# Regrouping a head's preparation: queries beside the gate tiles, keys and values beside an output projection

## The chip, the cores and the metric

The kernel runs on one core of one Trainium2 chip. The time is the device time of the program in microseconds (us), median of the runs taken. TensorE (PE) multiplies, ScalarE (ACT) and VectorE (DVE) copy, scale and reduce, GpSimd (POOL) does some elementwise work from SBUF, SyncE (SP) issues most transfers. Each engine takes its instructions in one fixed order.

## The reference

One decoder layer on 1024 tokens of width 1024, in float32, batch 1. Two branches read the same normalised input, and their outputs are projected by one matrix:

```python
h = rms_norm(x, norm1_g) * (1.0 + scale1) + shift1
q_lat, kv_lat, k_rope, x_lru, g_lru = jnp.split(h @ w_in, IN_SPLITS, axis=-1)
attn = mla_attention(q_lat, kv_lat, k_rope, ...)   # 4 heads, q and k normalised and rotated
lru = rg_lru_branch(x_lru, g_lru, ...)             # convolution, gates, scan, times gelu(g_lru)
mixed = jnp.concatenate([rms_norm(attn, ...), rms_norm(lru, ...)], axis=-1)
x = x + gate1 * (mixed @ w_out)
h2 = rms_norm(x, norm2_g) * (1.0 + scale2) + shift2
x = x + gate2 * hierarchical_moe(h2, ...)          # 32 experts, 2 per token
```

A head's query comes from `q_lat` through `w_q_b`, its key and value from `kv_lat` through `w_kv_b`; `k_rope` is shared by the heads.

## The kernel before

Tokens are handled as 8 tiles of 128 rows. `w_in` is multiplied in twelve column tiles (`FT`), each in two halves of 512 tokens; a float32 product is made of three faster ones (`mm3`: high by high, high by low, low by high), so one half of a tile is 24 PE instructions of 512 columns named `pp`. The last four tiles (i = 8 to 11) are the gate tiles `gl`: `gl_steps` multiplies them, and `gelu` (L654) makes the gate, multiplies it into the recurrent output `lru[j]` on DVE (L655), squares it on ACT (L659), and adds the square into `sqL` on POOL (L660).

Then `l_pass` projects the recurrent half of the mixed rows with rows 512 to 1023 of `w_out`. `out_w` loads four blocks `wo` of `w_out`, multiplies each by the gate row `m_g1` on POOL (L1046, four instructions a block), and splits it into `woh` (ACT) and `wol` (DVE, L222). `norms` sums `sqL` on PE (`pc2`, L1059) and takes a reciprocal root in twelve tiny DVE instructions (`rsq`, L199 to L213), which end in `ivL`. Sixteen output tiles `pL` of 12 PE instructions follow; each is scaled by `ivL` and added to the input rows `xr` by one DVE instruction (L1082) that also frees the PSUM bank. `pL` has three banks. A second `out_w` prepares the other half of `w_out` beside it, for the attention's projection much later.

`prep(h, P)` prepares a head. Its key part multiplies the latent by `w_kv_b` (24 PE instructions `pkv`, L225 to L227), copies keys (`kraw`, ACT) and values (`v`, DVE), squares, sums and takes a reciprocal root (`ssk`, `ik`), scales the keys on POOL (L807, L810) and transposes them twice (`k_t`, PE `ptk` and `ptk2`) into `kTh`, `kTl` and `ks`. Its query part multiplies by `w_q_b` (`pq`, L820), squares and rotates, and transposes (`ptq`) into `qTh`, `qTl`, `qs`, `ql`; a third `rsq` gives the scale `scq`.

For head 0 the whole of `prep` is written beside the end of `gl_steps` and `l_pass`, in turns that `merge` sets by two step counts; heads 1 to 3 are prepared beside the attention of the head before:

```python
gl = chain(gl_steps(), l_pass())
for _ in range(OPT["gl0"]):
    next(gl)
merge((gl, OPT["glw"] - OPT["gl0"]), (prep(0, P), NPREP))
drain(gl)
```

The written order is only a wish: a scheduler of the framework, which also gives out the buffers, fixes each engine's order when the program is built. With `phase(1)` the PSUM banks are given out anew; the first scores `pS` (L932) of head 0's attention follow.

Of the kernel before, what the change touches and what calls it, by code (L numbers as in the profile page):

```python
# [9 lines left out]
F32 = mybir.dt.float32  # L10
F32R = mybir.dt.float32r
# [3 lines left out]
AF = mybir.ActivationFunctionType  # L15
OP = mybir.AluOpType
# [122 lines left out]
def layer(ctx, tc, A, out, dbg=None, stop=None):  # L139
# [10 lines left out]
    def blk(name, dt=F32):  # L150
        return big.tile([128, 1024], dt, name=name, tag="b", bufs=NBLK)
# [77 lines left out]
    def t3(ap, t):  # L229
        return ap.rearrange("p (t f) -> p t f", t=t)  # L230
# [542 lines left out]
    attn = [None] * 4  # L773
    sqA = None

    def prep(h, P):
        kTh, kTl, ks = blk("kTh", F32R), blk("kTl", F32R), blk("ks", F32R)
        vh = blk("v")
        kraw = blk("kraw")
        P.update(kTh=kTh, kTl=kTl, ks=ks, v=vh)  # L780
        lkh, lkl = latk
        ssk = sm.tile([128, NT], F32, name="ssk")
        sq = blk("sqh")
        for t0 in range(0, NT, 2):
            pkk = t3(bank("pkv"), 2)
            for a in range(2):
                ts_ = slice((t0 + a) * 128, (t0 + a) * 128 + 128)
                hs = slice(h * 256, h * 256 + 256)
                mm3(pkk[:, a], lkh[:, ts_], lkl[:, ts_], wkh[:, hs], wkl[:, hs], True, True)
            for a in range(2):  # L790
                rk = r_k[:, t0 + a:t0 + a + 1]
                tk = slice((t0 + a) * 128, (t0 + a) * 128 + 128)
                SC.activation(kraw[:, tk], pkk[:, a, :128], AF.Copy, scale=rk)
                if OPT["ssk"]:
                    SC.activation(sq[:, tk], pkk[:, a, :128], AF.Square, scale=rk, accum_out=ssk[:, t0 + a:t0 + a + 1])
                V.tensor_scalar(vh[:, tk], pkk[:, a, 128:], rk, None, op0=OP.mult)
            yield
        if not OPT["ssk"]:
            SC.activation(sq, kraw, AF.Square)
            V.tensor_reduce(ssk, t3(sq, NT), op=OP.add, axis=AX.X)  # L800
            yield
        V.tensor_add(ssk, ssk, ssr)
        yield
        ik = sm.tile([128, NT], F32, name="ik")
        yield from rsq(ik, ssk, 1.0 / 192, EPS, [128, NT])
        k3 = t3(kraw, NT)
        G.tensor_mul(k3, k3, ik[:, :, None].to_broadcast([128, NT, 128]))  # L807
        kp3 = t3(sq, NT)
        for r in range(2):
            G.tensor_mul(kp3[:, :, r * 64:r * 64 + 64], krr, ik[:, :, None].to_broadcast([128, NT, 64]))  # L810
        yield
        ssh = sm.tile([128, NT], F32, name="ssh")
        Q = {}
        qst = {}

        def q_mm(t0):
            pq = t3(bank("pq"), 2)[:, :, :192]
            for a in range(2):
                for k in range(2):
                    T.matmul(pq[:, a], latq[k][:, (t0 + a) * 128:(t0 + a) * 128 + 128], wq[k][:, h * 192:(h + 1) * 192],  # L820
                             start=(k == 0), stop=(k == 1))
            qnp = half("qnp").rearrange("p (c a d) -> p c a d", c=2, a=2)
            qn, qp = qnp[:, 0], qnp[:, 1]
# [12 lines left out]
            two_ = lambda v: v[:, :, None, :].to_broadcast([128, 2, 2, 64])
            V.tensor_add(qp.rearrange("p a (r d) -> p a r d", r=2), two_(qp[:, :, 64:]), two_(tm))
            if not OPT["ssh"]:
                V.tensor_reduce(ssh[:, t0:t0 + 2], sqh, op=OP.add, axis=AX.X)
            qst[t0] = qn, qp  # L840

        def q_t(t0):
            qn, qp = qst.pop(t0)
            if t0 % 4 == 0:
                Q.update({n: half(n, F32R) for n in ("qTh", "qTl", "qs", "ql")})
                for n in Q:
                    P[n, t0 // 4] = Q[n]
                G.memset(Q["ql"][64:].bitcast(F32), 0.0)
            pt = bank("ptq")
            for a in range(2):  # L850
                T.transpose(pt[:, a * 128:(a + 1) * 128], qn[:, a], ident)
            for a in range(2):
                T.transpose(pt[:, 256 + a * 128:256 + (a + 1) * 128], qp[:, a], ident)
            tv = slice((t0 % 4) * 128, (t0 % 4) * 128 + 256)
            split(pt[:, :256], Q["qTh"][:, tv], Q["qTl"][:, tv])
            SC.activation(Q["qs"][:, tv], pt[:, 256:], AF.Copy)
            V.tensor_sub(Q["ql"][:64, tv], pt[:64, 256:], Q["qs"][:64, tv])

        def k_t(c0):
            tv = slice(c0 * 128, c0 * 128 + 512)  # L860
            pt = bank("ptk")
            for a in range(4):
                T.transpose(pt[:, a * 128:(a + 1) * 128], k3[:, c0 + a], ident)
            split(pt, kTh[:, tv], kTl[:, tv], scale=gg)
            yield
            pt = bank("ptk2")
            for a in range(4):
                T.transpose(pt[:, a * 128:(a + 1) * 128], kp3[:, c0 + a], ident)
            SC.activation(ks[:, tv], pt, AF.Copy)
            V.tensor_sub(ks[64:, tv], pt[64:], ks[64:, tv])  # L870
            yield

        def scale():
            sq_ = smc.tile([128, NT], F32, name="scq", bufs=2)
            r2 = sm.tile([128, NT], F32, name="r2")
            V.tensor_mul(r2, r_q, r_q)
            yield
            V.tensor_mul(r2, r2, ssh)
            yield
            yield from rsq(sq_, r2, 1.0 / 192, EPS, [128, NT])  # L880
            V.scalar_tensor_tensor(sq_, sq_, SCALE, r_q, op0=OP.mult, op1=OP.mult)
            yield
            nsq = smc.tile([128, NT], F32, name="nscq", bufs=2)
            V.tensor_scalar(nsq, sq_, -1.0, None, op0=OP.mult)
            P.update(scq=sq_, nscq=nsq)

        def turns():
            q_mm(0)
            yield
            for t0 in range(2, NT, 2):  # L890
                q_mm(t0)
                yield
                if t0 < NT - 2:
                    q_t(t0 - 2)
                    yield
                if t0 == 4:
                    yield from k_t(0)

        yield from turns()
        sc_ = scale()  # L900
        for f in (lambda: q_t(NT - 4), lambda: q_t(NT - 2)):
            f()
            yield
            for _ in range(4):
                next(sc_)
                yield
        for _ in k_t(4):
            yield
            for _ in range(3):
                next(sc_, None)  # L910
                yield
        yield from sc_
# [101 lines left out]

    def gl_steps():
        for i in range(8, 12):
            load_in(i + 2)
            for n in range(2):
                yield from project(i, n)
                evac(i, n)  # L1020
                if n == 0:
                    split_in(i + 2)
                yield
# [36 lines left out]
        drain(rsq(iv[:, ts[0]:ts[0] + n], pc[:, ts[0]:ts[0] + n], 1.0 / 512, EPS, [128, n]))  # L1060

    def l_pass():
        mod_row("g1", 2)
        yield from out_w([4, 5, 6, 7])
        norms(ivL, sqL, list(range(NT)))
        ow = out_w([0, 1, 2, 3])
        for g in range(4):
# [6 lines left out]
            for t in (2 * g, 2 * g + 1):  # L1074
# [700 lines left out]
```

## Time and profile before

| | |
|---|---|
| median of 3 runs | 814.96 us (814.83 to 815.29) |
| the profiled execution | 816.14 us |
| its span, first to last instruction | 814.4 us |
| PE busy | 730.2 us, 90% of the span |
| DVE busy | 447.6 us, 55% |
| ACT busy | 317.3 us, 39% |
| POOL busy | 157.6 us, 19% |
| mean granted TensorE clock | 0.975 |

The span is what the trace covers; 1.7 us of the profiled execution lie around it. The stretch that the change touches runs from about 186 us, when the gate tiles are multiplied, to 287.58 us, when PE starts the first scores. In the rows further down a number in brackets is the idle time just before an instruction, and behind the arrow stands what ended it.

### The profile page before, as it was taken

Reading aid. Unit: us, or ns where it says so; the run is one execution under the profiler, and the core shown is the slowest. Engines: PE = TensorE matmul, PEld = TensorE weight load, DVE = VectorE, ACT = ScalarE, POOL = GpSimd, SP = SyncE. Lnnn points to the kernel's source line nnn. Section 1 sums busy time; section 2 is a strip of 40 time slices with the busy share of each in tenths; the row PEclk is TensorE's granted clock in tenths of the full one; section 3 lists DMA queues with packets and bytes.
Section 4 is the critical chain, followed back from the end, with each engine's and each line's share of the span. In section 5 each row is a group of like instructions: output and inputs, shape, how many; then the busy total and the mean of one; then the engine's idle time right before and its main releaser. Section 6 shows DMA issues by size and latency. Waiting matters only on the chain. (4 is left out here: it accounts for less than half of the span.)

```text
span 814.4 us, 12262 instructions
## 1 busy us (share of the span) xinstructions
PE 730.2 (90%) x4257; PEld 470.3 (58%) x4257; DVE 447.6 (55%) x1334; ACT 317.3 (39%) x715; POOL 157.6 (19%) x150
## 2 busy tenths in 40 slices
PE   3799999989988989899999997699988789999994
PEld 1377776548876878788888886333233234333231
DVE  4597386869776468788884667434333122221311
ACT  3455456675344156667664444221201112120210
POOL 1121012102766102031311000212112111221101
PEclk9999999999999999999999998799989999999999
DMA  9952437682307403020154699899999999999993
GB/s 312 374 149 85 143 118 236 211 269 84 119 9 281 156 27 104 1 79 1 60 193 140 237 340 345 329 294 344 335 345 319 358 369 331 336 365 341 349 313 64
DMA packets 70976, 180.47 MB, mean 222 GB/s; under 512 B 8960, under 2 KB 22528, under 8 KB 70912
## 3 DMA queue, kind: packets, MB, share of 16 engines
q1 hardware_dynamic: 63328, 158.50, 54.9%
q0 software_dynamic: 7104, 21.00, 9.7%
q8 instruction: 34, 0.56, 0.3%
q10 hardware_dynamic: 480, 0.16, 0.1%
q14 instruction: 30, 0.25, 0.1%
HBM read 160.61 MB, written 22.95 MB: 225 GB/s over the span
## 5 line engine op out<-in xcount | busy, mean ns | idle before, releaser
L1649 PE MATMUL pgu<-ew,xeT 128*32 128x512 f32 (+1 forms) x928 | 166.4, 620 | 7.7 <-DMA ew<-in_w_e 7.5
L1649 PEld LDWEIGHTS pgu<-ew,xeT 128*32 128x32 f32 (+1 forms) x928 | 47.8, 122 | 100.2 <-issue 82.2
L1660 PE MATMUL py<-ew,hT 128*32 128x512 f32 (+1 forms) x464 | 78.5, 596 | 4.4 <-ACT hT L1634 4.4
L225 PE MATMUL pp<-hTh,winh 128*128 128x512 f32 x176 | 68.2, 400 | 5.8 <-DVE hTh L188 3.0
L226 PE MATMUL pp<-hTl,winh 128*128 128x512 f32 x176 | 70.1, 398 | 0.2 <-DVE hTl L469 0.2
L227 PE MATMUL pp<-hTh,winl 128*128 128x512 f32 x176 | 69.5, 396 | 0.0
L1663 DVE TENSOR_TENSOR y<-py,m_g 128x512 f32<-128x512 f32 (+1 forms) x40 | 27.6, 691 | 74.9 <-PE py L1660 70.0
L1623 ACT ACTIVATE sg<-pgu 128x256 f32<-128x256 f32 (+1 forms) x20 | 7.7, 386 | 130.4 <-PE pgu L1649 130.4
L1660 PEld LDWEIGHTS py<-ew,hT 128*32 128x32 f32 (+1 forms) x464 | 23.9, 120 | 49.8 <-issue 38.5
L1616 DVE TENSOR_SCALAR xeT<-pxe,gc,mc 128x128 f32<-128x128 f32 x80 | 27.4, 403 | 38.2 <-PE pxe L1610 38.2
L1634 ACT ACTIVATE hT<-pht 128x256 f32<-128x256 f32 (+1 forms) x20 | 7.6, 381 | 98.0 <-PE pht L1632 86.1
L1665 POOL DMA_INDIRECT out<-y,pki x13 | 20.7, 1594 | 115.4 <-DVE y L1663 91.3
L225 PEld LDWEIGHTS pp<-hTh,winh 128*128 128x128 f32 x176 | 33.4, 190 | 16.2 <-DVE hTh L188 4.0
L1625 DVE SCALAR_TENSOR_TENSOR hid<-sg,pkw,pgu 128x256 f32<-128x256 f32 (+1 forms) x13 | 6.2, 477 | 63.5 <-ACT sg L1623 63.5
L1614 ACT ACTIVATE xeT<-pxe,mc,gc 128x128 f32<-128x128 f32 x80 | 30.0, 461 | 25.9 <-PE pxe L1610 25.9
L226 PEld LDWEIGHTS pp<-hTl,winh 128*128 128x128 f32 x176 | 33.4, 190 | 9.9 <-issue 2.1
L227 PEld LDWEIGHTS pp<-hTh,winl 128*128 128x128 f32 x176 | 33.4, 190 | 8.3 <-DVE lq L587 0.8
L949 ACT ACTIVATE P<-pS,nb,scq 128x384 f32<-128x384 f32 (+2 forms) x48 | 32.3, 679 | 12.2 <-DVE nb L946 12.2
L983 PE MATMUL po<-PT,v 128*128 128x256 f32 (+1 forms) x160 | 35.8, 362 | 0.0
L1046 POOL TENSOR_TENSOR wo<-wo,m_g 128x256 f32<-128x256 f32 x32 | 28.2, 917 | 15.5 <-DMA wo<-in_w_out 15.5
L1610 PEld LDWEIGHTS pxe<-ident,xe 128*128 128x128 f32 x160 | 18.4, 145 | 21.0 <-issue 15.7
L983 PEld LDWEIGHTS po<-PT,v 128*128 128x128 f32 x160 | 28.8, 191 | 2.9
(424 smaller groups left out, 1615.0 us busy)
## 6 DMA issues: line engine op xcount, KB each, us to landing
ew<-in_w_e SPq DMA_DIRECT2D x186, 512.0 KB, 7.2
wad<-in_w_ada SPq DMA_DIRECT2D x64, 256.0 KB, 4.0
wada<-in_w_ada SPq DMA_DIRECT2D x16, 512.0 KB, 10.8
win<-in_w_in SPq DMA_DIRECT2D x12, 512.0 KB, 7.5
xt<-in_x SPq DMA_DIRECT2D x8, 512.0 KB, 6.6
wo<-in_w_out SPq DMA_DIRECT2D x8, 512.0 KB, 6.1
xr<-in_x SPq DMA_DIRECT2D x8, 512.0 KB, 4.6
x_d<-xr SPq DMA_DIRECT2D x8, 512.0 KB, 2.7
```

The lines of the kernel that those rows point to most:

```text
L225: T.matmul(o, lhi, rhi, start=first, stop=False)
L226: T.matmul(o, lhi, rlo, start=False, stop=False)
L227: T.matmul(o, llo, rhi, start=False, stop=last)
L949: SC.activation(Pt[:, o:o + w], pss[ci], AF.Exp, scale=P["scq"][:, i:i + 1], bias=nb, accum_out=l[:, ci:ci + 1])
L983: T.matmul(po[:, o:], P["v"][:, js], PT[j // 4][:, j % 4, o:], start=(j == 0), stop=(j == nj - 1), skip_group_check=True)
L1046: EN[OPT["g1"]].tensor_mul(w[:, q:q + 256], w[:, q:q + 256], mrow["g1"][:, q:q + 256])
L1614: SC.activation(xT[a][:, c], pt[:, c], AF.Identity, scale=gc[:, k:k + 1], bias=sh2[:, k:k + 1])
L1616: last["dve"] = V.tensor_scalar(xT[a][:, c], pt[:, c], gc[:, k:k + 1], sh2[:, k:k + 1], op0=OP.mult, op1=OP.add).ins
L1649: T.matmul(pg[r], xT[k // 4][:, c + r.start:c + r.stop], w[k // 2][:, NS[k % 2]], start=(k == 0), stop=(k == 7), skip_group_check=True)
L1660: T.matmul(py[n][r], hT[:, a * 128 + r.start:a * 128 + r.stop], w[4 + a][:, NS[n]], start=(a == 0), stop=(a == 1), skip_group_check=True)
L1663: last["dve"] = V.tensor_mul(y[:rows, NS[n]], py[n][:rows], mrow["g2"][:rows, NS[n]]).ins
L1665: G.indirect_dma_start(out=out, out_offset=bass.IndirectOffsetOnAxis(ap=idx, axis=0), in_=y[r0:r0 + idx.shape[0]], in_offset=None, compute ...
```

## The change

`prep` gets a third argument that says which parts it makes: the queries (`"q"`), the keys and values (`"k"`), or both as before. Head 0's queries are now written in turns with the last 18 steps of `gl_steps`, and its keys and values in turns with `l_pass`; the two transposes `k_t(0)` and `k_t(4)` come last of all. The load of the gate row and of the first four blocks of `w_out` moves in the text from the start of `l_pass` to the start of the last gate tile. Heads 1 to 3 are prepared as before.

```diff
-    def prep(h, P):
-        kTh, kTl, ks = blk("kTh", F32R), blk("kTl", F32R), blk("ks", F32R)
...
+    def prep(h, P, only="kq"):
         lkh, lkl = latk
...
+        def keys():
+            nonlocal kTh, kTl, ks, k3, kp3
+            kTh, kTl, ks = blk("kTh", F32R), blk("kTl", F32R), blk("ks", F32R)
...
-                if t0 == 4:
+                if t0 == 4 and "k" in only:
                     yield from k_t(0)
 
+        if "k" in only:
+            yield from keys()
+        if only == "k":
+            yield from k_t(0)
+            yield from k_t(4)
+            return
         yield from turns()
...
-        for _ in k_t(4):
+        for _ in k_t(4) if "k" in only else ():
             yield
...
     def gl_steps():
         for i in range(8, 12):
+            if i == 11:
+                mod_row("g1", 2)
+                next(ow_l)
             load_in(i + 2)
...
     def l_pass():
-        mod_row("g1", 2)
-        yield from out_w([4, 5, 6, 7])
+        for _ in ow_l:
+            yield
...
+    ow_l = out_w([4, 5, 6, 7])
...
-    gl = chain(gl_steps(), l_pass())
-    for _ in range(OPT["gl0"]):
+    gl, lp_ = gl_steps(), l_pass()
+    for _ in range(6):
         next(gl)
-    merge((gl, OPT["glw"] - OPT["gl0"]), (prep(0, P), NPREP))
-    drain(gl)
+    merge((gl, 18), (prep(0, P, "q"), 18))
+    merge((lp_, 24), (prep(0, P, "k"), 18))
```

Three places show how it moves the engines' own orders. The first is POOL, from the first squares of the gate tiles to the end of head 0's preparation; `wo` are the blocks of `w_out`, `kraw` and `sqh` the keys to be scaled. Before:

```order
L660 TENSOR_TENSOR sqL<-sqL,gelu 128x512 x3
L1046 TENSOR_TENSOR wo<-wo,m_g_1940 128x256 x8
L807 TENSOR_TENSOR kraw<-kraw,ik 128x1024
L810 TENSOR_TENSOR sqh<-krr,ik 128x8x64 x2
L1046 TENSOR_TENSOR wo<-wo,m_g_1940 128x256 x4
L660 TENSOR_TENSOR sqL<-sqL,gelu 128x512
L1046 TENSOR_TENSOR wo<-wo,m_g_1940 128x256 x4
L660 TENSOR_TENSOR sqL<-sqL,gelu 128x512
L848 MEMSET ql 64x512
L660 TENSOR_TENSOR sqL<-sqL,gelu 128x512
L848 MEMSET ql 64x512
L1046 TENSOR_TENSOR wo<-wo,m_g_1940 128x256 x16
```

Of the change, on POOL from the same place on:

```order
L660 TENSOR_TENSOR sqL<-sqL,gelu 128x512
L1059 TENSOR_TENSOR wo<-wo,m_g_1924 128x256 x8
L852 MEMSET ql 64x512
L1059 TENSOR_TENSOR wo<-wo,m_g_1924 128x256 x8
L660 TENSOR_TENSOR sqL<-sqL,gelu 128x512 x5
L1059 TENSOR_TENSOR wo<-wo,m_g_1924 128x256 x16
L811 TENSOR_TENSOR kraw<-kraw,ik 128x1024
L814 TENSOR_TENSOR sqh<-krr,ik 128x8x64 x2
```

All sixteen multiplications of the first four blocks now stand ahead of the last five squares, and the keys of head 0 are scaled behind all 32 instead of behind the first eight. On SP the loads of the second four `wo` blocks, which stood behind the first two stores of finished rows (L1086), now stand ahead of all of them.

The second place is DVE, ahead of the first `pL` tile that it takes out of PSUM (`xr`). Before:

```order
L213 SCALAR_TENSOR_TENSOR rs_y<-rs_t,rs_y 128x8 x2
L209 TENSOR_TENSOR rs_t<-rs_y 128x8 x2
L211 SCALAR_TENSOR_TENSOR rs_t<-rs_t,rs_x 128x8 x2
L213 SCALAR_TENSOR_TENSOR ivL<-rs_t,rs_y 128x8
L213 SCALAR_TENSOR_TENSOR scq<-rs_t,rs_y 128x8
L1082 SCALAR_TENSOR_TENSOR xr<-pL,ivL,xr 128x512
```

Of the change, on DVE, the last rows ahead of the same instruction (now L1095):

```order
L806 TENSOR_TENSOR ssk<-ssk,ssr 128x8
L211 SCALAR_TENSOR_TENSOR rs_t<-rs_t,rs_x 128x8
L219 TENSOR_TENSOR mLl<-gt_wa,mLh 128x256
L199 TENSOR_SCALAR rs_x<-ssk 128x8
L219 TENSOR_TENSOR mLl<-gt_wa,mLh 128x256
L213 SCALAR_TENSOR_TENSOR ivL<-rs_t,rs_y 128x8
L219 TENSOR_TENSOR mLl<-gt_wa,mLh 128x256
L202 TENSOR_SCALAR rs_i<-rs_x 128x8
L219 TENSOR_TENSOR mLl<-gt_wa,mLh 128x256 x3
L205 TENSOR_SCALAR rs_y<-rs_i 128x8
L219 TENSOR_TENSOR mLl<-gt_wa,mLh 128x256
L1095 SCALAR_TENSOR_TENSOR xr<-pL,ivL,xr 128x512
```

The low halves `mLl` of the first three groups of rows (twelve instructions, before only the first four) and the start of the keys' root now stand ahead of the first `xr`. From the copy `v` that frees the last bank for `pkv` to this `xr` the new order has one `wol`, four more `v`, twelve `mLl`, sixteen tiny ones and one reduction.

The third place is PE, from the last `pL` instructions to the first scores. Before:

```order
L225 MATMUL pL<-woh,mLh 128x512
L226 MATMUL pL<-wol,mLh 128x512
L227 MATMUL pL<-woh,mLl 128x512
L932 MATMUL pS<-kTh,qTh 128x256
L933 MATMUL pS<-kTl,qTh 128x256
```

Of the change, on PE at the same place:

```order
L225 MATMUL pL<-woh,mLh 128x512
L226 MATMUL pL<-wol,mLh 128x512
L227 MATMUL pL<-woh,mLl 128x512
L867 MATMUL ptk<-ident,kraw 128x128 x3
L872 MATMUL ptk_2476<-ident,sqh 128x128 x4
L867 MATMUL ptk<-ident,kraw 128x128 x4
L872 MATMUL ptk_2490<-ident,sqh 128x128 x4
L942 MATMUL pS<-kTh,qTh 128x256
```

Fifteen of the sixteen key transposes moved from among the `pL` instructions to behind the last of them. The second `ptk` group waits for DVE's `kTl` of the first, and the first score for DVE's `ks` of the second.

## Rows read from the trace of the kernel before

**Rows 1.** Stretches: busy us of PE, PEld, DVE, ACT, POOL; granted clock, DMA share, GB/s

```profile
200.00:223.20 23.20, 23.20 (x109) 19.46 (x108) 17.04 (x29) 10.46 (x19) 15.97 (x16) 1.00 0.36 131
223.20:235.30 12.10, 8.61 (x45) 7.98 (x44) 7.76 (x15) 7.22 (x21) 11.96 (x11) 0.86 0.09 35
235.30:261.90 26.60, 23.95 (x122) 19.51 (x121) 20.28 (x65) 10.64 (x30) 11.05 (x14) 1.00 0.55 198
```

**Rows 2.** PE's timeline, 223 to 236 us: start, duration, engine, line, operation [idle before]

```profile
223.23 2.76 PE L820 MATMUL pq<-wq,latq 128*128 128x192 f32 x16
228.00 0.44 PE L851 MATMUL ptq<-ident,qnp 128*128 128x128 f32 x2 [2.01 <-ACT qnp L824]
229.92 2.49 PE L820 MATMUL pq<-wq,latq 128*128 128x192 f32 x8 [1.48 <-DVE qtmp L835]
232.63 2.03 PE L820 MATMUL pq<-wq,latq 128*128 128x192 f32 x8
...
235.30 0.48 PE L225 MATMUL pL<-woh,mLh 128*128 128x512 f32 x1
```

**Rows 3.** The same timeline, 250 to 288 us: PE's other holes, and the last pL

```profile
250.18 0.44 PE L851 MATMUL ptq<-ident,qnp 128*128 128x128 f32 x2 [0.98 <-DVE ks L870]
...
251.41 0.50 PE L225 MATMUL pL<-woh,mLh 128*128 128x512 f32 x1 [0.58 <-ACT mLh L218]
...
261.96 0.50 PE L225 MATMUL pL<-woh,mLh 128*128 128x512 f32 x1 [1.16 <-DVE xr L1082]
...
286.35 0.39 PE L227 MATMUL pL<-woh,mLl 128*128 128x512 f32 x1
287.58 0.39 PE L932 MATMUL pS<-kTh,qTh 128*128 128x256 f32 x1 [0.84 <-DVE xr L1082]
```

**Rows 4.** One short stretch, columns as in rows 1: the slow clock

```profile
231.00:233.00 2.00, 2.00 (x9) 1.91 (x8) 0.16 (x1) 0.55 (x1) 2.00 (x3) 0.50 0.00 0
```

**Rows 5.** PE's timeline: the first of twelve pkv, and the instruction behind them

```profile
203.63 0.28 PE L225 MATMUL pkv<-wkh,latkh 128*128 128x256 f32 x1
...
205.06 0.40 PE L227 MATMUL pp<-hTh,winl 128*128 128x512 f32 x1
```

**Rows 6.** DVE's timeline: tiny root steps, v, mLl, xr and wol at several times

```profile
205.19 1.62 DVE L796 TENSOR_SCALAR v<-pkv,r_k 128x128 f32<-128x128 f32 x4 [0.95 <-ACT kraw L793]
...
212.21 0.65 DVE L209 TENSOR_TENSOR rs_t<-rs_y 128x8 f32<-128x8 f32 x1
...
226.41 0.69 DVE L655 TENSOR_TENSOR gt_wa<-gt_wa,gelu 128x512 f32<-128x512 f32 x1 [1.18 <-ACT gelu L654]
...
251.43 1.41 DVE L219 TENSOR_TENSOR mLl<-gt_wa,mLh 128x256 fp32r<-128x256 f32 x4
...
261.16 2.06 DVE L1082 SCALAR_TENSOR_TENSOR xr<-pL,ivL,xr 128x512 f32<-128x512 f32 x3
...
267.55 1.28 DVE L222 SCALAR_TENSOR_TENSOR wol<-wo,col,woh 128x1024 fp32r<-128x1024 f32 x1 [1.00 <-ACT woh L221]
...
319.61 0.17 DVE L209 TENSOR_TENSOR rs_t<-rs_y 128x8 f32<-128x8 f32 x1
```

**Rows 7.** POOL's timeline: two runs of the wo multiplications

```profile
211.42 5.60 POOL L1046 TENSOR_TENSOR wo<-wo,m_g 128x256 f32<-128x256 f32 x8
...
254.92 11.40 POOL L1046 TENSOR_TENSOR wo<-wo,m_g 128x256 f32<-128x256 f32 x12 [4.05 <-DMA wo<-in_w_out]
```

**Rows 8.** Timelines of PE, ACT and DVE: one key transpose and what follows

```profile
244.95 0.60 PE L863 MATMUL ptk<-ident,kraw 128*128 128x128 f32 x4
...
245.59 0.69 ACT L221 ACTIVATE kTh<-ptk,gg 128x512 fp32r<-128x512 f32 x1 [1.26 <-PE ptk L863]
...
246.31 0.75 DVE L222 SCALAR_TENSOR_TENSOR kTl<-ptk,gg,kTh 128x512 fp32r<-128x512 f32 x1 [0.41 <-ACT kTh L221]
...
249.43 0.69 DVE L870 TENSOR_TENSOR ks<-ptk,ks 64x512 fp32r<-64x512 f32 x1 [0.32 <-ACT ks L869]
```

More of the change, by code (lines that the diff above doesn't have):

```diff
@@ L774, in layer @@
     sqA = None
-    def prep(h, P):
-        kTh, kTl, ks = blk("kTh", F32R), blk("kTl", F32R), blk("ks", F32R)
-        vh = blk("v")
-        kraw = blk("kraw")
-        P.update(kTh=kTh, kTl=kTl, ks=ks, v=vh)
-        lkh, lkl = latk
[L782 to L796, printed above, removed]
-            yield
-        if not OPT["ssk"]:
-            SC.activation(sq, kraw, AF.Square)
-            V.tensor_reduce(ssk, t3(sq, NT), op=OP.add, axis=AX.X)
-            yield
[L802 to L811, printed above, removed]
@@ new lines, in prep @@
+    def prep(h, P, only="kq"):
+        lkh, lkl = latk
+        kTh = kTl = ks = k3 = kp3 = None
+        def keys():
+            nonlocal kTh, kTl, ks, k3, kp3
+            kTh, kTl, ks = blk("kTh", F32R), blk("kTl", F32R), blk("ks", F32R)
+            vh = blk("v")
+            kraw = blk("kraw")
+            P.update(kTh=kTh, kTl=kTl, ks=ks, v=vh)
+            ssk = sm.tile([128, NT], F32, name="ssk")
+            sq = blk("sqh")
+            for t0 in range(0, NT, 2):
+                pkk = t3(bank("pkv"), 2)
+                for a in range(2):
+                    ts_ = slice((t0 + a) * 128, (t0 + a) * 128 + 128)
+                    hs = slice(h * 256, h * 256 + 256)
+                    mm3(pkk[:, a], lkh[:, ts_], lkl[:, ts_], wkh[:, hs], wkl[:, hs], True, True)
+                for a in range(2):
+                    rk = r_k[:, t0 + a:t0 + a + 1]
+                    tk = slice((t0 + a) * 128, (t0 + a) * 128 + 128)
+                    SC.activation(kraw[:, tk], pkk[:, a, :128], AF.Copy, scale=rk)
+                    if OPT["ssk"]:
+                        SC.activation(sq[:, tk], pkk[:, a, :128], AF.Square, scale=rk, accum_out=ssk[:, t0 + a:t0 + a + 1])
+                    V.tensor_scalar(vh[:, tk], pkk[:, a, 128:], rk, None, op0=OP.mult)
+                yield
+            if not OPT["ssk"]:
+                SC.activation(sq, kraw, AF.Square)
+                V.tensor_reduce(ssk, t3(sq, NT), op=OP.add, axis=AX.X)
+                yield
+            V.tensor_add(ssk, ssk, ssr)
+            yield
+            ik = sm.tile([128, NT], F32, name="ik")
+            yield from rsq(ik, ssk, 1.0 / 192, EPS, [128, NT])
+            k3 = t3(kraw, NT)
+            G.tensor_mul(k3, k3, ik[:, :, None].to_broadcast([128, NT, 128]))
+            kp3 = t3(sq, NT)
+            for r in range(2):
+                G.tensor_mul(kp3[:, :, r * 64:r * 64 + 64], krr, ik[:, :, None].to_broadcast([128, NT, 64]))
+            yield
@@ L1062, in l_pass @@
     def l_pass():
-        mod_row("g1", 2)
-        yield from out_w([4, 5, 6, 7])
+        for _ in ow_l:
+            yield
         norms(ivL, sqL, list(range(NT)))
```

## The prediction

> **What bounds the kernel now.** Start with the table of stretches [rows 1]. While the gate tiles are multiplied (200 to 223.2 us) PE is busy all the time, 23.20 of 23.20 us: no rearrangement can make that stretch faster, only fill it with other work. In the next 12.1 us PE is busy for 8.61 and its clock stands at 0.86. Then look at PE's timeline: between the last gate instruction, about 223.4, and the first `pL` at 235.30 only head 0's query products run, with holes of 2.01 and 1.48 us [rows 2]; at 231 to 233 the clock is at 0.50, the lower of its two levels (1.2 GHz), after those holes [rows 4]. Four more holes follow, 0.98, 0.58, 1.16 and 0.84 us, the last one just ahead of the first scores [rows 3]. Everything before and after is dense or, by each engine's order, unchanged: behind the first few scores the rows of all five engines are the same. So I compare one moment, the start of the first scores, 287.58 us before [rows 3], and pass its shift on to the end one for one.
>
> **What could be won.** The holes are 2.01 + 1.48 + 0.98 + 0.58 + 1.16 + 0.84 = 7.05 us, and the slow clock costs 12.1 x (1 - 0.86) = 1.7 us [rows 1 to 3]. PE's products themselves are the same, so 8.8 us is all there is, and the change keeps it only as far as it makes no holes of its own.
>
> **Step 1: the gate stage with the queries in it.** The 24 `pkv` products leave it: twelve take 205.06 - 203.63 = 1.43 us, so 2.9 [rows 5]. The 32 query rows come in, 16 of them in 2.76 us [rows 2], so 5.5, and 16 query transposes at about 0.1 each (four of a kind take 0.60 with the tail of the last [rows 8]), 1.6. The stage ends at 223.4 + 4.2 = 227.6. I cost its holes at nothing: ACT is busy for 10.46 of 23.20 us there and DVE for 17.04 [rows 1], the keys' copies leave them, and PE has 10 to 40 gate products in its order between a query's product and the transpose that needs it. If that cover fails, see the third rival.
>
> **Step 2: from the last gate product to the first `pL`.** Now the 24 key products stand there, and they wait for PSUM banks that DVE frees. The recurrent product of the last gate starts at 226.41 before, 3.0 us behind the last gate product, and takes 0.69 [rows 6]; ACT has less in front of it now, so it is done 1.5 to 3.7 us behind, at 229.1 to 231.3. Behind it in DVE's order stand two `wol` at 1.28 and four `v` at 0.40 before the last bank is free [rows 6], 4.2 us, plus up to 1.3 for POOL's squares (below); then six key products, 0.7 [rows 5]. `pL` starts at 234.0 to 237.5. I take 235.5: the ends are set by the ACT queue and the middle assumes that half its delay is gone. Before it was 235.3. **The gain of the first two holes and of the clock is spent here**, since the gate's last results now hold the key banks up, where the query products used to run without them.
>
> **Step 3: the first `pL` tiles must leave PSUM.** Three banks hold 36 products. At 0.23 each (108 of them run from 261.96 to 286.35 without a hole [rows 3]) PE is through with them 8.2 us behind the start. It then waits for the first `xr`. From the last `v` of step 2, 0.75 us ahead of the first `pL`, DVE has in its order: one `wol` 1.28, four `v` 1.6, twelve `mLl` at 0.35 is 4.2, sixteen tiny root steps at 0.2 (0.17 and a gap [rows 6]) is 3.2, a reduction over 1024 columns that I count like a `wol`, 1.3 (an estimate), and the `xr` itself 0.69. Sum 12.3, so PE waits 12.3 - 0.75 - 8.2 = 3.3 us at least.
>
> That holds with POOL silent. At 212.21 the same tiny step takes 0.65 instead of 0.17 us, while POOL runs `wo` multiplications of 5.60 / 8 = 0.70 each [rows 6, 7]: the two take turns. The `xr` row does not slow down in POOL's other run, 0.69 each at 261.16, and there POOL's multiplications stretch to 0.95 [rows 6, 7]. So what waits is DVE's instructions with two operands in SBUF. The Trainium skill has this in "SBUF — State Buffer", section "Who interferes with whom": such an instruction and a GpSimd one that reads SBUF exclude each other for the whole instruction. By that rule each of POOL's sixteen could hold one DVE instruction up for its full 0.70, 11.2 us in all, and the wait of this step would be 14.5. The rows agree on who waits, and the sum below goes by them.
>
> Where is POOL at that time? Its second sixteen multiplications stood at 248 to 266 because their loads were queued on SP behind the stores of finished rows; now the loads stand ahead of the stores, and POOL reaches them right behind the last square, at about 233. They last at least 16 x 0.70 = 11.2 us, that is over the very twelve microseconds of DVE's chain to the first `xr`. Of the chain 22 instructions have two operands in SBUF (twelve `mLl`, ten tiny). A tiny one loses 0.65 - 0.17 = 0.5, and until POOL is through some ten of them and half the `mLl` meet it: 10 x 0.5 at least is 5, less if POOL is late, more if the `mLl` wait as long. I take 4.7, bounds 0 and 8. Step 3 then costs a hole of **8.0 us** (3.3 to 11).
>
> **Step 4: the keys' transposes at the end.** Fifteen of them now stand behind the last `pL`. From that product's start: 0.23 to the next, 0.60 for the transposes, 0.69 ACT, 0.75 DVE, then again 0.60, 0.69, 0.75 for the second four tiles, and 0.69 for DVE's last `ks` [rows 8]: 5.0 us with the `ks` of ACT in the shadow, where 287.58 - 286.35 = 1.2 stood [rows 3]. With gaps of 0.04 between engines 5.2; bounds 4.5 and 5.5.
>
> **The sum.** 235.5 + 191 x 0.228 = 43.5 to the last `pL`, + 8.0 + 5.2 + 0.2 for the one transpose in between = 292.4, against 287.58: **+4.8 us**. The clock fell before behind holes of 2.01 and 1.48 with little between them [rows 2, 4]; a hole of 8 us should do the same to the `pL` behind it, 1.7 us again, and behind the tail of step 4 a further 0 to 1.7 that I leave out. **+6.5 us.** On the span of 814.4 that is 820.9; the profiled execution (816.14) has 1.7 us around the span and lies 1.2 above the median, so on the median: 814.96 + 6.5 = **821.5**.
>
> **The rivals.**
> *The stage closes up (faster).* POOL's second loads land late or its turns miss DVE's chain: a wait of 3.3 in step 3, `pL` from 234.0, no slow clock, as all of PE's holes then are short. 234.0 + 43.5 + 3.3 + 5.2 + 0.2 = 286.2, 1.4 earlier; with a hole of 2.3, if ACT is early too, 2.4 earlier: 812.6 to 813.6. It decides on the start of POOL's second run: behind 240 us this rival wins. The Trainium skill's "Perfetto Trace Analysis", section "Matmul Optimizations", speaks for it: the matmul engine scales with its use, so products should stand back to back. By that rule the query products, now between gate products, lose their slow stretch. The rows of the old stretch agree, but the new holes are longer than the old ones.
> *No change.* Turns cost little (3.3), `pL` from 235.5, no slow clock: 287.7, that is 815.1.
> *Worse.* The queries' chain on ACT and DVE makes holes in the gate stage, as it does at 228 and 229.9 [rows 2], 3.5 us more, and the clock falls twice: 821.5 + 3.5 + 1.7 = 826.7. For it: all sixteen first multiplications of POOL run in that stage too, beside the scale's tiny steps. Against it: ten and more gate products between the steps.
> That the change doesn't reach the engines' orders is out: the rows of the orders show it.
>
> **How the numbers follow.** Forecast (+3 to +10) 0.57, worse 0.16, no change 0.12, faster 0.15. A difference of 0.2%, 1.6 us, is about what can be told from none. Slower 0.73, within 0.12, faster 0.15. The range leaves out the better half of the faster case and the outer half of the worse one: 813.3 to 826.5.
>
> **What would show it.** Right: no PE hole of over 1 us before 227; the first `pL` at 234 to 237; one hole of 5 to 11 us about 36 products later, released by DVE's `xr`, with tiny DVE steps of 0.65 beside a POOL run of sixteen; a granted clock near 0.5 for some microseconds behind it; PE idle for 3 to 4 us in the 5 before the first scores, released by DVE's `ks`. Wrong: POOL's run behind 240, or a first `xr` within 9 us of the first `pL`; the first scores at or before 287.

## The result, and the profile after

The changed kernel is slower: 822.08 us (median of five runs, 820.64 to 824.39) against 814.83 us of the kernel before in the same measurement, ratio **1.008** with a 95% interval of 1.0054 to 1.0106, some 7.2 us more. The prediction was 821.5 us. The profiled execution took 820.64 us, with a span of 818.9.

The first table answers [rows 1] and [rows 4]: stretches of the changed kernel, with the busy us of PE, PEld, DVE, ACT and POOL (instructions in brackets), then the granted clock, the DMA share and GB/s.

```profile
200.00:223.20 23.20, 23.20 (x118) 19.73 (x117) 18.38 (x43) 11.22 (x35) 15.77 (x20) 1.00 0.12 40
223.20:235.30 12.10, 10.15 (x61) 8.98 (x60) 9.44 (x12) 9.43 (x20) 7.62 (x6) 0.96 0.71 262
235.30:261.90 26.60, 21.17 (x81) 17.05 (x80) 23.83 (x53) 10.13 (x20) 16.78 (x19) 0.83 0.30 118
...
234.40:237.50 3.10, 3.10 (x10) 2.72 (x11) 3.10 (x5) 1.43 (x5) 3.10 (x4) 0.50 1.03 422
250.40:254.40 4.00, 3.92 (x9) 3.14 (x10) 3.77 (x13) 0.42 (x1) 0.00 (x0) 0.50 0.32 131
...
293.10:299.00 5.90, 5.87 (x26) 5.68 (x27) 1.52 (x6) 2.82 (x6) 0.00 (x0) 0.50 0.00 0
```

The gate stage is as full as before. The 12.1 us behind it have become better, 10.15 us busy instead of 8.61. A part of the loss stands in the third line: 21.17 of 26.60 busy where it was 23.95, at a clock of 0.83 instead of 1.00. The last three lines are the stretches at the lower clock level (0.50, that is 1.2 GHz); the last of them lies among the scores, where the kernel before ran at 1.00.

PE's timeline of the changed kernel answers [rows 2, 3]; columns as there.

```profile
179.38 0.50 PE L225 MATMUL pp<-hTh,winh 128*128 128x512 f32 x1 [0.84 <-ACT krT L636]
...
227.82 0.39 PE L227 MATMUL pp<-hTh,winl 128*128 128x512 f32 x1
228.05 0.28 PE L225 MATMUL pkv<-wkh,latkh 128*128 128x256 f32 x1
...
232.42 0.36 PE L225 MATMUL pkv<-wkh,latkh 128*128 128x256 f32 x1 [1.64 <-DVE v L800]
...
235.79 0.63 PE L225 MATMUL pL<-woh,mLh 128*128 128x512 f32 x1
...
244.66 0.39 PE L227 MATMUL pL<-woh,mLl 128*128 128x512 f32 x1
250.47 0.79 PE L225 MATMUL pL<-woh,mLh 128*128 128x512 f32 x1 [5.43 <-DVE xr L1095]
...
287.90 0.39 PE L227 MATMUL pL<-woh,mLl 128*128 128x512 f32 x1
...
290.19 0.66 PE L867 MATMUL ptk<-ident,kraw 128*128 128x128 f32 x4 [1.13 <-DVE kTl L222]
...
293.13 0.58 PE L942 MATMUL pS<-kTh,qTh 128*128 128x256 f32 x1 [1.56 <-DVE ks L874]
...
313.12 0.47 PE L942 MATMUL pS<-kTh,qTh 128*128 128x512 f32 x1
```

Three new waits stand where the old ones were: 1.64 us ahead of a key product, 5.43 us behind the first 36 `pL`, and 1.13 + 1.56 us in the tail between the last `pL` and the first scores. The stretch from the last `pL` to the first score, called the tail below, is 293.13 - 287.90 = 5.23 us; it was 1.23.

DVE's and POOL's timelines of the changed kernel between the first `pL` and the first `xr` answer [rows 6, 7]:

```profile
235.82 2.43 DVE L219 TENSOR_TENSOR mLl<-gt_wa,mLh 128x256 fp32r<-128x256 f32 x3
...
239.68 0.34 DVE L800 TENSOR_SCALAR v<-pkv,r_k 128x128 f32<-128x128 f32 x1
239.94 0.52 DVE L205 TENSOR_SCALAR rs_y<-rs_i 128x8 int32<-128x8 int32 x1
240.49 0.66 DVE L209 TENSOR_TENSOR rs_t<-rs_y 128x8 f32<-128x8 f32 x1
...
244.58 1.21 DVE L804 TENSOR_REDUCE ssk<-sqh 128x8 f32<-128x1024 f32 x1
...
246.96 0.15 DVE L211 SCALAR_TENSOR_TENSOR rs_t<-rs_t,rs_x 128x8 f32<-128x8 f32 x1
247.04 0.41 DVE L219 TENSOR_TENSOR mLl<-gt_wa,mLh 128x256 fp32r<-128x256 f32 x1
...
249.68 0.74 DVE L1095 SCALAR_TENSOR_TENSOR xr<-pL,ivL,xr 128x512 f32<-128x512 f32 x1
```

```profile
233.03 13.65 POOL L1059 TENSOR_TENSOR wo<-wo,m_g 128x256 f32<-128x256 f32 x16
254.52 1.90 POOL L811 TENSOR_TENSOR kraw<-kraw,ik 128x1024 f32<-128x1024 f32 x1 [7.85 <-DVE ik L213]
```

POOL's run ends at 246.7. Until then a tiny step takes 0.66 us and an `mLl` 0.81 (three in 2.43); behind it the same two kinds take 0.15 and 0.41. The values `v`, which come out of PSUM, and the reduction take the same beside POOL as without it.

**A yardstick.** Single runs of one kernel spread over 1% (the kernel before: 810.3 to 820.6 us in all measurements of this study), and the traces put most of that into the last 500 us, where the work is the same: from the second score product of 512 columns to the end it takes 508.5 us in the trace before, 505.8 in the one after, and 502.5 to 511.6 in those of the experiments. So beside the ratio each kernel is read by one interval in its trace, from the input product that waits for `krT` to that score product. Before:

```profile
179.34 0.50 PE L225 MATMUL pp<-hTh,winh 128*128 128x512 f32 x1 [0.84 <-ACT krT L636]
...
305.95 0.48 PE L932 MATMUL pS<-kTh,qTh 128*128 128x512 f32 x1
```

That is 126.6 us before and 313.12 - 179.38 = 133.7 after: **+7.1 us**, which agrees with the medians. Only 1.5 of them are there at the last `pL`, where the gate stage's gain has paid for most of the hole; 4.0 come in the tail and 1.6 behind it. A second trace of the changed kernel (experiment 10) gives 134.4, so differences of under 1 us between two traces are not read.

### The profile page after: what moved, and what is told of

The parts are those of the page before. It is cut to its first block, busy times and chain, and to the rows that moved or that the text cites. A ratio compares the mean times of both kernels' runs of the same rounds, so it can differ in the third digit from the quotient of the medians.

```text
span 818.9 us, 12265 instructions
## 1 busy us (share of the span) xinstructions
PE 733.1 (90%) x4257; PEld 474.7 (58%) x4257; DVE 454.0 (55%) x1334; ACT 316.9 (39%) x715; POOL 154.2 (19%) x150
## 5 line engine op out<-in xcount | busy, mean ns | idle before, releaser
L1664 PE MATMUL pgu<-ew,xeT 128*32 128x512 f32 (+1 forms) x928 | 163.5, 605 | 8.6 <-DMA ew<-in_w_e 8.5
L225 PE MATMUL pL<-woh,mLh 128*128 128x512 f32 x64 | 26.7, 417 | 5.4 <-DVE xr L1095 5.4
```

The costliest lines, as they stand in the source:

```text
L225: T.matmul(o, lhi, rhi, start=first, stop=False)
L1664: T.matmul(pg[r], xT[k // 4][:, c + r.start:c + r.stop], w[k // 2][:, NS[k % 2]], start=(k == 0), stop=(k == 7), skip_group_check=True)
```

## The experiments

Every kernel, with its interval; "first score" is also counted from the `krT` product. Of 7, 8 and 11 there is one run each, and only its trace is read.

| kernel | first score | interval | against before | ratio (95%) |
|---|---|---|---|---|
| before | 108.2 | 126.6 | | |
| changed | 113.8 | 133.7 | +7.1 | 1.008 (1.0054 to 1.0106) |
| 1 transposes among the `pL` | 112.3 | 130.6 | +4.0 | 1.0076 (1.0045 to 1.0108) |
| 2 second `wo` whole behind the keys | 107.3 | 141.5 | +14.9 | 1.0165 (1.0128 to 1.0201) |
| 3 both | 106.3 | 130.6 | +3.9 | 1.0033 (1.0011 to 1.0055) |
| 4 keys in the gate stage too | 125.4 | 143.8 | +17.2 | 1.0192 (1.0152 to 1.0231) |
| 5 both, loads early | 103.7 | 122.0 | -4.6 | 0.9929 (0.9903 to 0.9955) |
| 6 as 5, first `wol` early | 103.2 | 121.6 | -5.0 | 0.9903 (0.9876 to 0.993) |
| 7 first `wol` early alone | 112.4 | 131.9 | +5.3 | |
| 8 before, second `wo` early | 111.8 | 130.2 | +3.6 | |
| 9 POOL late, tail kept | 106.6 | 125.5 | -1.1 | 0.9981 (0.9959 to 1.0003) |
| 10 changed, again | 114.4 | 134.4 | +7.8 | 1.0083 (1.0051 to 1.0115) |
| 11 third part undone | 113.8 | 132.6 | +6.0 | |

The theory: the change loses by two things, POOL's second run beside DVE's chain to the first `xr`, and the key transposes behind the last `pL`; behind both the clock falls in its trace.

### Experiment 1: the tail alone

```diff
-    merge((lp_, 24), (prep(0, P, "k"), 18))
+    merge((islice(lp_, 16), 24), (prep(0, P, "k"), 18))
+    drain(lp_)
```

> The changed kernel, with the key transposes written ahead of the last four output tiles; every engine's order up to there is unchanged, so the wait of 5.43 us for the first xr stays. Theory (the tail costs): in the changed kernel the first scores start 293.13 - 287.90 = 5.2 us behind the last pL product, before it was 1.2. With the transposes hidden that is 1.2 again, 4.0 us less, and the granted clock should stay at 1.00 behind it, where the changed kernel runs 292 to 299 at 0.54 to 0.60: some 2.5 us more. So 822.1 - 6.5 = 815.6. Rival 1 (the clock gives nothing back): 822.1 - 4.0 = 818.1. Rival 2 (the copies of the transposes on DVE and ACT only make new waits among the last tiles): 821 to 822.

PE's timeline of this kernel:

```profile
249.87 0.80 PE L226 MATMUL pL<-woh,mLh 128*128 128x512 f32 x1 [4.16 <-DVE xr L1096]
...
278.02 0.66 PE L868 MATMUL ptk<-ident,kraw 128*128 128x128 f32 x4 [1.13 <-DVE kTl L223]
...
289.66 0.39 PE L228 MATMUL pL<-woh,mLl 128*128 128x512 f32 x1
290.99 0.36 PE L943 MATMUL pS<-kTh,qTh 128*128 128x256 f32 x1 [0.94 <-DVE xr L1096]
```

The tail is 1.33 us, 3.9 less, as expected, and the scores behind it run at a clock of 1.00, which is worth 1.6 us (from the first score to the end of the interval 18.3 us instead of 20.0). The wait for the first `xr` is shorter than in the changed kernel, 4.16 for 5.43, because PE comes to it later: the `pL` product behind it starts 71.1 us behind the `krT` product in both, as DVE sets it. The interval is only 3.1 us shorter. The wait of 1.13 for `kTl` came along, since both banks of the transposes are taken, and the transposes, which ran in the tail's waits for nothing, now take PE's own time. So the theory's 6.5 us were twice too many, and a part of rival 2 came true, a new wait among the last tiles; the ratio alone, 1.0076, does not tell this kernel from the changed one.

### Experiment 2: POOL's run alone, with its loads

```diff
-            G.tensor_mul(k3, k3, ik...)
+            P["kmul"] = G.tensor_mul(k3, k3, ik...)
...
-        ow = out_w([0, 1, 2, 3])
...
-            if g == 1:
-                next(ow)
...
-                    if g > 1:
-                        next(ow, None)
...
     merge((lp_, 24), (prep(0, P, "k"), 18))
+    with tc.issue_after(P["kmul"].ins):
+        drain(out_w([0, 1, 2, 3]))
```

> The changed kernel, with the second four wo blocks multiplied on POOL only behind the scaling of the keys, so that POOL is silent while DVE works towards the first xr; the twelve mLl, the root steps and the reduction still stand ahead of that xr, and the transposes still stand last. Theory (turns with POOL make the hole): beside POOL the mLl took 0.81 instead of 0.35 us and the tiny steps 0.44 to 0.67 instead of 0.17; summed over the chain that is 5 to 6 us. The hole of 5.43 us falls to 0 to 0.5, the granted clock behind it stays at 1.00 (2 us more): 822.1 - 7.2 = 814.9. Rival (DVE's longer order is enough by itself, 3.3 us by the prediction's sum): the hole stays at 3.3 us, the clock still falls: 822.1 - 2.1 = 820.0.

The hole of 5.43 us is gone and the first score stands 6.5 us earlier, as the theory said; yet the kernel is much slower. PE's timeline, then ACT's, of this kernel:

```profile
306.19 0.45 PE L980 MATMUL ptP<-ident,P 128*128 128x128 f32 x1 [14.39 <-ACT kraw L797]
```

```profile
290.19 1.15 ACT L221 ACTIVATE woh<-wo,col 128x1024 fp32r<-128x1024 f32 x1 [4.92 <-POOL wo L1059]
...
301.49 1.15 ACT L221 ACTIVATE woh<-wo,col 128x1024 fp32r<-128x1024 f32 x1 [2.61 <-POOL wo L1059]
302.54 0.60 ACT L797 ACTIVATE kraw<-pkv,r_k 128x128 f32<-128x128 f32 x2
```

The edit had moved the loads as well, to behind the stores on SP. POOL multiplied at 287.4 to 301.5, and ACT, in its fixed order, stood at the four `woh` with the next head's `kraw` and the exponentials of the scores behind them. The expectation had left out who waits for POOL's results.

### Experiment 3: both

The edit of experiment 2, with the `merge` of experiment 1 cut at 14 steps.

> Both edits at once: the second wo blocks multiplied behind the scaling of the keys, the key transposes written among the output tiles. Theory (the two losses lie one behind the other on PE and add up): 822.1 - 6.5 - 7.2 = 808.4, faster than before by some 6 us. Rival (one wait hides the other, as the keys come later or earlier with POOL's order): not below 812.

A miss by the same flaw: POOL's run at 276.9 to 291.0, a wait of 2.08 us ahead of the first score and of 5.10 behind it. The first scores nevertheless start 2.0 us ahead of the kernel before.

### Experiment 5: both, with the loads left early

```diff
-            G.tensor_mul(k3, k3, ik...)
+            P["kmul"] = G.tensor_mul(k3, k3, ik...)
...
-                    if g > 1:
-                        next(ow, None)
+                    if "kmul" in P:
+                        with tc.issue_after(P["kmul"].ins):
+                            next(ow, None)
...
-    merge((lp_, 24), (prep(0, P, "k"), 18))
+    merge((islice(lp_, 14), 24), (prep(0, P, "k"), 18))
+    drain(lp_)
```

> The changed kernel with the key transposes written among the output tiles, the second wo blocks loaded as early as in the changed kernel, and only their multiplications on POOL put behind the scaling of the keys. In the third experiment the loads had moved too, POOL multiplied at 276.9 to 291.0, and ACT's and DVE's halves of these blocks made a hole of 2.08 us ahead of the first scores and one of 5.10 behind them. Theory (that was all that was left): POOL multiplies at about 253 to 265 beside xr steps that do not slow down; from the last gate product to the first scores 57.8 - 1.2 = 56.5 us, where the kernel before took 64.6 with a gate stage about 4.5 shorter, that is 3 to 3.5 us ahead of the kernel before, ratio 0.996. Rival (ACT waits for POOL's blocks and holds the key copies up): ratio 0.999 to 1.002.

PE's, POOL's and DVE's timelines:

```profile
236.30 0.63 PE L226 MATMUL pL<-woh,mLh 128*128 128x512 f32 x1
...
282.24 0.39 PE L228 MATMUL pL<-woh,mLl 128*128 128x512 f32 x1
283.56 0.36 PE L943 MATMUL pS<-kTh,qTh 128*128 128x256 f32 x1 [0.94 <-DVE xr L1096]
```

```profile
247.71 1.90 POOL L812 TENSOR_TENSOR kraw<-kraw,ik 128x1024 f32<-128x1024 f32 x1 [14.32 <-issue]
...
251.57 11.18 POOL L1060 TENSOR_TENSOR wo<-wo,m_g 128x256 f32<-128x256 f32 x16
```

```profile
236.11 1.08 DVE L220 TENSOR_TENSOR mLl<-gt_wa,mLh 128x256 fp32r<-128x256 f32 x3
...
244.07 0.74 DVE L1096 SCALAR_TENSOR_TENSOR xr<-pL,ivL,xr 128x512 f32<-128x512 f32 x1
```

No hole stands between the first `pL` and the last. POOL's run, now beside `xr` steps, takes 11.18 us instead of 13.65. The kernel is 0.7% faster than the kernel before, more than the theory's 0.4%: the change has a gain once its two losses are taken out.

### Experiment 9: POOL late, the tail kept

```diff
-            G.tensor_mul(k3, k3, ik...)
+            P["kmul"] = G.tensor_mul(k3, k3, ik...)
...
         if only == "k":
+            with tc.issue_after(P["kmul"].ins):
+                drain(P["ow"])
             yield from k_t(0)
...
-        ow = out_w([0, 1, 2, 3])
+        ow = P["ow"] = out_w([0, 1, 2, 3])
...
-                    if g > 1:
-                        next(ow, None)
```

> The changed kernel with one edit: POOL multiplies the second wo blocks behind the scaling of the keys, with their loads as early as in the changed kernel. DVE's order up to the first xr is that of the changed kernel, row for row; nine key transposes stay behind the last pL. Theory (POOL's run is the whole cause of the 5.43 us hole, and the slow clock behind it 1.9 us more): no hole at the first xr, the tail still 4.5 to 5.5 us with the slow clock behind it (1.6), first scores 6.5 to 7.5 us earlier than the changed kernel, about 286; ratio to the kernel before 0.998 to 1.001. Rival (part of the hole belongs to the order of DVE): a hole of 1.5 us or more stays, first scores at 288 or later, ratio 1.003 or more.

DVE's timeline, then PE's:

```profile
236.15 1.08 DVE L219 TENSOR_TENSOR mLl<-gt_wa,mLh 128x256 fp32r<-128x256 f32 x3
...
238.47 0.17 DVE L209 TENSOR_TENSOR rs_t<-rs_y 128x8 f32<-128x8 f32 x1
...
242.81 1.09 DVE L219 TENSOR_TENSOR mLl<-gt_wa,mLh 128x256 fp32r<-128x256 f32 x3
...
244.23 0.74 DVE L1097 SCALAR_TENSOR_TENSOR xr<-pL,ivL,xr 128x512 f32<-128x512 f32 x1
```

```profile
282.41 0.40 PE L227 MATMUL pL<-woh,mLl 128*128 128x512 f32 x1
...
286.45 0.38 PE L944 MATMUL pS<-kTh,qTh 128*128 128x256 f32 x1 [1.41 <-DVE ks L874]
```

The order of DVE up to the first `xr` is the changed kernel's, row for row, and no hole is left. From the first `mLl` to the end of the first `xr` DVE takes 244.97 - 236.15 = 8.8 us (8.7 in experiment 5), where the changed kernel needs 250.42 - 235.82 = 14.6. So POOL's run costs this chain 5.8 to 5.9 us, and without it the `xr` comes before PE asks for its bank: the longer order of DVE makes no hole by itself, and the rival falls. At the last `pL` this kernel is 6.0 us ahead of the changed one, counted from the `krT` product. The other 2.2 of its 8.2 us lie behind: the tail is 4.0 us, since six more transposes found a place among the `pL`, and the low clock behind it takes 1.0 less.

With experiments 1 and 5 there are two pairs for each loss. By the interval POOL's place is worth 8.2 us with the tail and 8.6 without, the transposes 3.1 with POOL early and 3.5 with POOL late: within what two traces of one kernel differ by, the two add up. The pairs are not clean, as the number of moved transposes differs.

### Experiment 8: POOL's run in the kernel before

```diff
-            if g == 1:
+            if g == 0:
                 next(ow)
```

> The kernel before, with the second wo blocks loaded one group of rows earlier in the text, so that POOL multiplies them right behind the first sixteen, beside the root steps that end in ivL; nothing else is edited. Theory (turns with POOL are a cause by themselves): the 24 root steps ahead of the first xr take 0.65 us instead of 0.17 while POOL runs, the first xr comes 5 to 10 us later, PE waits 2 to 7 us, the first scores start at 289.5 to 295 instead of 287.6. Rival (the hole needs the changed kernel's longer DVE order): first scores at 287 to 288.5.

PE's timeline, then POOL's:

```profile
251.00 0.80 PE L225 MATMUL pL<-woh,mLh 128*128 128x512 f32 x1 [3.63 <-DVE xr L1082]
```

```profile
237.71 11.94 POOL L1046 TENSOR_TENSOR wo<-wo,m_g 128x256 f32<-128x256 f32 x16
```

One number in the text brings such a hole into the kernel before, and 3.6 us with it. From the first `mLl` to the end of the first `xr` DVE now takes 14.8 us, 7.2 before, with most tiny steps at 0.5 to 0.8 us while POOL runs. The scheduler also moved other rows: the first `pL` starts 1.7 us later, and two of the old holes are gone, so the 3.6 us are not the hole alone. But POOL's place makes a hole here without the regrouped preparation.

### Experiment 4: the keys beside the gate tiles too

```diff
-    merge((gl, 18), (prep(0, P, "q"), 18))
-    merge((lp_, 24), (prep(0, P, "k"), 18))
+    merge((gl, 18), (prep(0, P, "q"), 18), (prep(0, P, "k"), 22))
+    drain(lp_)
```

> The changed kernel with the keys, too, written beside the gate tiles, and the output projection alone behind them. Theory (the gate stage's gain is spent because key products wait there for banks that DVE frees): the 24 key products (2.9 us) and 16 transposes (1.6 us) move into the gate stage without holes, its end goes from 228.05 to about 232.5; the first pL then waits only for the last gate's ACT and DVE work, 3 us, with no key copies in between, so it starts at about 235.5 as in the changed kernel, but the tail (5.2 us) is gone and the chain to the first xr is shorter by eight v and a reduction: 822.1 - 4.0 - 2 to 5 = 813 to 816. Rival (DVE and ACT are full in the gate stage, holes appear there): holes of 2 to 5 us before 232, time 818 to 821.

Worse than either theory. PE's, DVE's and ACT's timelines:

```profile
233.28 0.79 PE L225 MATMUL pp<-hTh,winh 128*128 128x512 f32 x1 [7.28 <-ACT gelu L654]
```

```profile
217.42 0.17 DVE L209 TENSOR_TENSOR rs_t<-rs_y 128x8 f32<-128x8 f32 x1
...
221.02 1.61 DVE L199 TENSOR_SCALAR rs_x<-r 128x8 f32<-128x8 f32 x1
...
224.93 0.66 DVE L209 TENSOR_TENSOR rs_t<-rs_y 128x8 f32<-128x8 f32 x1
```

```profile
232.35 0.38 ACT L860 ACTIVATE qs<-ptq 128x256 fp32r<-128x256 f32 x1 [7.09 <-DVE qTl L219]
```

The root of the queries' scale ran beside POOL's scaling of the keys and its `wo` blocks, 10.6 us for its twelve tiny steps (221.02 to 231.58), where nine of the keys' root had taken 1.8 with POOL silent (217.01 to 218.79). Behind it in DVE's order stood `qTl`, behind that in ACT's order the `gelu` that frees a bank for the gate products, and PE stood for 7.28 us in a stage that had no hole. That is less than half of the 17.2 us. A wait of 4.57 us for the first `xr` came again, with POOL's second run beside DVE's chain (250.6 to 264.8), and waits of 0.98, 1.91 and 2.50 lie ahead of the `pL`. This is the prediction's third rival, "Worse", in another kernel.

### Experiments 7 and 6: the first wol in the gate stage

```diff
             for n in range(2):
+                if i == 11:
+                    next(ow_l)
+                    next(ow_l)
                 yield from project(i, n)
```

Experiment 7 has this edit alone, experiment 6 has it on top of experiment 5 (with the cut at 12 steps).

> The changed kernel with wol in the last gate tile alone; POOL's second run stays beside DVE's chain to the first xr, and the transposes stay last. Theory: the chain of seven mLl, two v and twelve root steps takes some 5 us with POOL silent and 10 beside it; first xr 12 to 14 us behind the last gate product, PE through with its first 36 pL and the keys by then, a hole of 1 to 4 us; the tail of 5.2 us is there: 59 to 62 us from the last gate product to the first scores, 4 to 6 more than in the sixth kernel. Rival (turns with POOL cost nothing where the chain starts earlier): no hole, 57 to 58.

> The fifth kernel, and the low halves wol of the first wo blocks written into the last gate tile, so that they no longer stand between the values v that free the banks for the key products; the scheduler now puts nine pL ahead of the keys. Theory (the old place of wol spends the gate stage's gain): pL starts 3 to 4 us behind the last gate product (8.0 in the changed kernel), key products and transposes lie among the pL, no hole ahead of the first xr: 3.5 + 43.5 + 2.9 + 1.6 + 1.2, and 2 for the clock behind the first hole, is 54.7 us to the first scores, 5 ahead of the kernel before: ratio 0.993 to 0.995. Rival (the key products now wait between pL for banks, DVE's v stand behind the first xr): two or three holes of 1 to 2 us and the slow clock, ratio 0.997 to 1.0.

In both the first `pL` follows the last gate product at once, 0.2 us behind it, not 3 to 4: its nine first products need only the gates that were done earlier. In experiment 7 POOL's run then makes holes of 0.76 and 2.62 us, released by DVE's `v` and `xr`, and the tail is 5.3; from the last gate product to the first scores it takes 64.0 us, more than the 59 to 62 expected. Experiment 6 takes 54.8, as expected, and is the fastest kernel of the study, 0.9903. Against experiment 5 the interval is only 0.4 us shorter and the 95% intervals of the ratios overlap: no worth of the place of `wol` by itself is shown. Of the 7.9 us that the ratio of experiment 6 gives, 2.9 lie outside the interval and are not explained.

### Experiments 11 and 10: the third part, and the change again

In experiment 11 `mod_row("g1", 2)` and the first step of `ow_l` stand again at the start of `l_pass`.

> The changed kernel with the third part of the change undone: gate row and first four wo blocks are again written at the start of the projection. Theory (this part carries nothing of the result): POOL still multiplies the first blocks from about 207 to 222 and the second right behind the squares, the hole at the first xr is 4 to 7 us, the tail 5.2; first scores at 292 to 294.5. Rival (the early first blocks are what brings POOL's second run into DVE's chain): the hole falls to under 2 us, first scores at 289 or earlier.

PE's timeline:

```profile
251.36 0.80 PE L225 MATMUL pL<-woh,mLh 128*128 128x512 f32 x1 [4.87 <-DVE xr L1093]
...
293.36 0.38 PE L942 MATMUL pS<-kTh,qTh 128*128 128x256 f32 x1 [1.57 <-DVE ks L874]
```

A hole of 4.87 us, POOL's second run at 233.11, first scores at 293.36: the early load of the gate row is not the cause. The tail is the same as in the changed kernel, 5.23 us with waits of 1.13 and 1.57. Yet the clock behind it stays at 1.00, and from the first score to the end of the interval it takes 18.7 us instead of 20.0.

> The changed kernel itself, beside the others on one chip. By the trace its scores are 7.2 us late at 313.12 (third long score) against 305.95 before, hole, tail and slow clock together: ratio 1.007 to 1.010. If the runs of the kernel before on this chip spread as in the first experiments, the interval is some 0.3% to either side.

PE's timeline:

```profile
251.00 0.80 PE L225 MATMUL pL<-woh,mLh 128*128 128x512 f32 x1 [4.26 <-DVE xr L1095]
```

Ratio 1.0083 and an interval of 134.4 us: the result repeats. The hole is 4.26 us here, not 5.43. The clock fell one group of key products sooner, so the first `pL` starts 1.1 us later; the product behind the hole starts 71.1 us behind the `krT` product in both traces.

## Why the prediction was right

**Step 1** said that the gate stage ends at 227.6 without holes: the first key product starts at 228.05, and PE is busy for all of 23.20 us. **Step 2** said 235.5 for the first `pL`: 235.79. Its mechanism held, the key products wait for `v` behind `wol` (1.64 us); but the clock falls there already, and the first five `pL` cost some 1.0 us more, which was not in the sum.

**Step 3** had the right wait, releaser and cause, and POOL's second run came when it said, at 233.03. The size was wrong: 8.0 us forecast, 5.43 and 4.26 measured in two traces. Three terms were off. DVE's chain without POOL was put at 12.3 - 0.75 = 11.5 us behind the first `pL`; experiments 9 and 5 show 8.8 and 8.7 from the first `mLl`, which starts with the first `pL` in the changed kernel. The error is in the prices: the 0.40 of a `v` was the mean of a merged row with waits inside, where a `v` behind another costs 0.27; a tiny step between two others costs 0.1; and the `wol` was done before the first `pL`. POOL's part was put at 4.7 us and is 5.8 to 5.9, inside the bounds. And PE came through its 36 products 9.1 us behind their start, not 8.2, by the slow clock. "3.3 us at least, with POOL silent" was wrong: with POOL silent there is no wait at all.

The Trainium skill's rule ("SBUF — State Buffer", "Who interferes with whom") was right about who waits: not `v` from PSUM, not the reduction, but steps with two operands in SBUF; it also lets a `TENSOR_SCALAR` between SBUF tiles wait, which the prediction did not count and the trace shows (0.52 us for `rs_y`, 0.16 behind POOL's run). The 14.5 us worked out from it as an upper case did not come: POOL's sixteen instructions cost DVE's chain 5.8 to 5.9 us, not 11.2.

**Step 4** said 5.2 us for the tail: 5.23, with PE idle for 2.7 us of it and not 3 to 4. **The clock** was put at 1.7 us behind the hole, and 0 to 1.7 behind the tail were left out of the sum. Measured in the changed kernel's trace: 1.0 at the first `pL`, 1.9 behind the hole (nine products in 4.0 us instead of 2.1), and 1.6 at the scores behind the tail. The last is no fixed price, as experiment 11 has the same tail, a clock of 1.00 and only 0.4 behind it.

Together, at the first scores: the forecast was +6.5 with its clock. The first `pL` came 0.3 later, the hole was 2.6 shorter, and the clock cost 1.2 more (2.9 for 1.7), which makes +5.4; +5.5 was measured. With the 1.6 behind the tail it is +7.1, and the medians say +7.2. So a hole that was forecast 2.6 us too long hid a clock that was forecast 2.8 us too cheap. The two losses and their causes were foreseen, but that 821.5 lies so near to 822.08 is luck. That the first scores' shift goes on to the end one for one was wrong by just this 1.6.

The rival **"The stage closes up"** named the right sign: in experiment 9 POOL's run starts at 252.2, behind the 240 named, and the hole is gone. Its price is near, but not by its terms: 1.4 to 2.4 us less were forecast, and 1.5 by the ratio (0.9981, an interval that takes in 1) and 1.1 by the trace were measured, with no wait where it had 2.3 to 3.3, a first `pL` some 3 us later than its 234.0, and a low clock where it had none. **"Worse"** appeared in experiment 4 alone. **The gain** that the change could keep was put at 8.8 us at most; experiments 5 and 6 keep 4.6 and 5.0 us by the interval, 5.8 and 7.9 by the ratio.

## What to carry to other kernels

Look at what GpSimd does beside a chain of small VectorE steps on which TensorE waits: the same run of multiplications cost some 6 us beside that chain and made no wait beside the `xr` steps some 18 us later. When a step is moved off one engine's way, follow its results too, the engine that consumes them stands in its own fixed order (experiment 2). And price the clock behind each new wait of TensorE, the end of a stage included, as a range: behind the same two waits it was low in experiment 10 and full in experiment 11.

## What the runs showed of the hardware

A tiny VectorE step of 128 x 8 can cost almost ten times its 0.17 us: beside GpSimd multiplications of some 0.7 us it took 0.66, beside one of 1.9 us (`kraw`, 220.70 to 222.61 in experiment 4) it took 1.61. GpSimd loses as well, but to the larger steps: its sixteen multiplications take 11.2 us in experiment 5 beside `xr`, 13.65 beside that chain, and 14.6 in experiment 9 beside `wol` and `mLl`. Of the sixteen in the changed kernel the two that met a `wol` took 1.5 and 1.7 us, the four beside `mLl` 0.91, and those beside the tiny steps 0.74, as in experiment 5.

A wait of about 1 us behind dense work left the clock at 1.00 (0.94 us in experiment 1, ahead of the scores). Behind the tail's two waits of 1.13 and 1.56 us the changed kernel ran 5.9 us at 0.50, its second trace (experiment 10) 3.6 us at 0.54, and experiment 11, with the same two waits, at 1.00. Why they differ is open.
